# Attention on one core: the value products of a tile's two heads in turn, and scores, maxima, exponentials and scalings branch by branch

## The chip, the cores and the metric

The kernel runs on 1 core of one Trainium2 chip. The metric is the device time of one execution in microseconds (us), as the median of several runs. Lower is better.

## The reference, cut to what matters

Two layers on 256 tokens of width 1024: an HGRN2 mixer with its feed-forward, then a sparse attention (16 query heads of 64, 4 key heads, three branches) with its feed-forward. Everything is float32. With 256 tokens all blocks are selected and the window covers everything, so the selected and the windowed branch are plain causal attentions with keys and values of their own; the third branch attends to 15 compressed blocks.

```python
s_s = jnp.einsum('bqhgd,bhqkd->bhgqk', qr, ks_g) * scale
p_s = masked_softmax(s_s, m_s[:, :, None])
o_s = jnp.einsum('bhgqk,bhqkd->bqhgd', p_s.astype(vs_g.dtype), vs_g)
...
p_w = masked_softmax(s_w, m_w)
o_w = jnp.einsum('bhgqk,bkhd->bqhgd', p_w.astype(vw.dtype), vw)
o = g[:, :, 0] * o_c + g[:, :, 1] * o_s + g[:, :, 2] * o_w
```

## The kernel before, in words

Weights come from HBM as one stream of chunks of 1 MB (tile `raw`, four buffers). Most chunks are split into a high and a low part (`wh` on ScalarE, `wl` on VectorE), and each product is three fp32r matmuls (L484 to L486 in `gemm`). The conditioning vectors are products of plain float32 chunks with column tiles of 32 (`adapsg`, `adapsss`, L385); a scheduler puts them between the pieces of the attention.

The attention works on 8 tiles of two heads. A tile's two heads lie on partitions 0 to 63 and 64 to 127, and are called first and second head (`half` 0 and 1). The branches `br` 0 and 1 are the selected and the windowed one, `tt` is the half of the tokens.

`attend_scores(j)`, L1195: for each half of the tokens and each head one score product into a PSUM bank of its own (tile `s`, L1207), with 64 contracted rows; it holds both branches. Then VectorE adds the mask and takes the maxima (L1211, into `Pt` and `mx`), ScalarE takes eight exponentials (called at L1220, recorded at L429) and VectorE scales by the gate over the sum (L1229).

`attend_values(j)`, L1232: for each of the four pairs of head and branch, three 128x128 transposes through PSUM (`ptt`, L1244) and a copy to `PT` (VectorE for the first, L1247; ScalarE for the others, L1249). Then ten products go into one bank `po`, the first head's to its partitions 0 to 63, the second head's to 64 to 127: per head one of 256 columns with the compressed values (`PC`, L1256) and, per branch, one of 256 (L1260) and one of 128 columns (L1262). The stationary operand is 128 rows by 64 columns, so a product fills half of TensorE's columns; `tile_position` names which half. The trace calls such a shape 128\*64. A float32 product runs as two passes, each with a weight load of its own: the trace has two records for one matmul. Last, `po` is split into `hh` and `hl` (L479, L480) for the output product `nso`.

The order of the calls is a table (`ORDER["nsa"]`), but each engine's order is made by a scheduler that follows the order of the program with an offset (`@first("av")` moves the values forward). The banks `s`, `po` and some others share four PSUM buffers (tag `m`), the transposes share three (tag `acc`), `PT` has five buffers.

Of the kernel before, what the change touches and what calls it, by code (L numbers as in the profile page):

```python
# [20 lines left out]
P = 128  # L21
S = 256
D = 1024
# [4 lines left out]
RAW = 4  # chunks loaded ahead  # L28
DEFER = 3  # chunks of a feed-forward's first product taken before rstd is there
XBUFS = 14  # L30
XMOD, XOFF = 5, 9  # every how many halves of a chunk go to the second ring, and until which chunk
PTS = 3  # pairs of heads with probabilities at a time
QACT, KACT = 0x0F, 0xF0  # chunks of the queries' and values' input made on ACT
CSTK = 7  # chunk after which the rest of the constants is loaded
# how far ahead of the program (behind it, if negative) some of the work is issued
PRI = {"gates": -100, "av": 10, "res": 60, "rot": -15, "fh": 60}
EPS = 1e-6
# [5 lines left out]


# conditioning vectors (s shift and scale, g gate) on the tensor engine; the others are row sums on DVE
# [11 lines left out]
# The order of the work. hgrn: D decays, S scores, i/g products, V values. nsa: q queries, G gates, c compression,  # L57
# n norms, w values, x compressed softmax, s scores, v outputs, a conditioning chunk.
# hada, f0, f1: after how many chunks of products each conditioning chunk comes.
# [115 lines left out]
def row_constants():  # L175
    """Row 32 m + h of column block m: ones on the partitions of half h."""
    r = np.zeros((P, 4, P), np.float32)
    for m in range(4):
        for h in range(2):
            r[32 * m + h, m, 64 * h:64 * h + 64] = 1.0  # L180
    return r.reshape(P, 4 * P)


def first(name):
    """What the method issues is moved by PRI in the order of the program."""
    def wrap(f):
        def g(self, *a, **k):
            n = PRI.get(name, 0)
            if not n:
                return f(self, *a, **k)  # L190
            with self.tc.high_priority(offset=n):
                return f(self, *a, **k)
        return g
    return wrap


class K:
# [154 lines left out]
    def ada(self, kind, l, i, t):  # L352
        """Two columns of 128 conditioning values: rows of the chunk against c."""
        nc = self.nc
# [19 lines left out]
    def ada_pe(self, kind, l, i, t):  # L374
        """c against the chunk's rows, summed over the chunks; at the last one the columns."""
        nc = self.nc
# [42 lines left out]
    def act(self, out, in_, func, **kw):  # L419
        """An activation whose function lies in a table set; sets change only between phases."""  # L420
# [17 lines left out]
    def rsqrt_cols(self, v, n, tag):  # L438
        """v ** -0.5 for a few columns, by Newton's method from the exponent."""
# [11 lines left out]
    def rsqrt(self, v, shape, tag):  # L451
        """(v + EPS) ** -0.5, one Newton step after the tables."""
# [13 lines left out]
    def sigmoid(self, out, v, shape):  # L466
        """exp(min(v, 0)) / (1 + exp(-|v|))"""
# [26 lines left out]
    def gemm(self, ps, w, hh, hl, n=256):  # L494
        """ps = sum over k of w[k] (128 x 128) against h[:, k, :n]."""
# [3 lines left out]
    def tiles(self, w):  # L499
        """The 128 x 128 tiles of half a chunk: high and low parts."""  # L500
# [7 lines left out]
    def set_shift(self, hh, hl, l):  # L508
        """Columns 256 and 257 of the moving operand: the shift vector and zeros."""
# [14 lines left out]
    def stat(self, x, m):  # L524
        """Adds the squares of chunk m to the sum over chunks."""
# [10 lines left out]
    def first_stat(self):  # L536
        """rstd of the input."""
# [25 lines left out]
    def stat_end(self, ps=None):  # L563
        """self.rstd = (mean of squares + EPS) ** -0.5 of every token, on all partitions."""
# [17 lines left out]
    def full_chunk(self, hh, hl, m, A, sh, pool):  # L582
        """Chunk m of x * rstd * A + shift, in two parts."""
# [7 lines left out]
    def full_pair(self, which, l, xr, pool, on_act):  # L591
        """The same from x * rstd."""
# [22 lines left out]
    def gemm_deferred(self, ws, h, pool, name, ub=2):  # L615
        """Products with h as it is before rstd: their values times rstd, and the shift's column."""
# [17 lines left out]
    def residual(self, ps, m, gate, nxt):  # L634
        """x_new chunk m = x + gate * y, with what the next products need of it."""
# [20 lines left out]
    def hgrn(self):  # L656
# [3 lines left out]
        with self.tc.tile_pool(name="hg", bufs=1) as gp, self.tc.tile_pool(name="hg2", bufs=2) as g2:  # L660
# [17 lines left out]
            # room of the next operands until their first parts are there  # L678
# [62 lines left out]
    def gemm_tok(self, ps, h, ws):  # L741
        """Tokens on the partitions: h (stationary) against the weights."""
# [9 lines left out]
    def hgrn_decays(self, fs, qs, g2):  # L752
        """X[l]: exp of the log decay from each block's middle; left keys, right queries. X[8]: keys."""
# [41 lines left out]
    def hgrn_scores(self, X, q, g2, i):  # L795
        nc = self.nc
        # scores inside blocks of 32, all levels side by side
# [45 lines left out]
    def hgrn_values(self, ns, As, v, g2, q):  # L843
        """Into q: rms-normalised rows of A^T v times the gain, features on the partitions."""
# [75 lines left out]
    def raw_heads(self, ps, name):  # L920
        """Products of two column tiles off the accumulator, and their squares."""
# [7 lines left out]
    def rotate(self, u, gain, swap, kr, name):  # L929
        """kr = the rotation of u times the gain: halves of a head change places."""  # L930
# [11 lines left out]
    def head_norm(self, pairs, kr, gain=None, kn=None):  # L942
        """Four column tiles: kr times the heads' rstd, kn = u times that and the gain."""
        nc = self.nc
        ps = self.m_tile([P, S], "hs")
        # rows 32 e and 32 e + 1: the two heads of column tile e
# [124 lines left out]
    def cmp_blocks(self, sw, u, kind, Dt, pool):  # L1071
        """Dt[(parity, d), i, (head, block)]: token 16 block + 2 i + parity of a head, plus its position."""
# [122 lines left out]
    def attend_scores(self, j):  # L1195
# [7 lines left out]
        for tt, (o, n) in enumerate(((0, P), (P, S))):  # L1203
            for half in range(2):
                hs = slice(64 * half, 64 * half + 64)
                ps = self.m_tile([P, 2, n], f"s{tt}")
                nc.tensor.matmul(ps, lhsT=self.QR[hs, j, tt * P:tt * P + P], rhs=self.KR[hs, g, :, 0:n],  # L1207
                                 start=True, stop=True)
                for br in range(2):
                    i = half * 4 + br * 2 + tt  # L1210
                    nc.vector.tensor_tensor_reduce(out=Pt[half][:, br, o:o + n], in0=ps[:, br], in1=cs[:, S - n:],  # L1211
# [4 lines left out]
        for half in range(2):  # L1216
            for br in range(2):
# [8 lines left out]
        for half in range(2):  # L1226
            for br in range(2):
# [5 lines left out]
    def attend_values(self, j):  # L1233
# [4 lines left out]
        for half in range(2):  # L1238
            for br in range(2):
                PT[half, br] = self.pt_tile(f"PT{j}_{half}{br}")  # L1240
                pt = self.pp.tile([P, 3, P], F32, tag="acc", bufs=3, name="ptt")
                # columns: keys 0 with tokens 0, keys 0 with tokens 1, keys 1 with tokens 1
# [8 lines left out]
        for half in range(2):  # L1251
            hs = slice(64 * half, 64 * half + 64)
            kv = 2 * g + half
            o = po[hs]
            tpos = (0, 64 * half)
            nc.tensor.matmul(o, lhsT=self.VC[:, g, (j % 4) * 2 + half], rhs=self.PC[g].rearrange("p a b -> p (a b)"),  # L1256
                             start=True, stop=False, tile_position=tpos)
            for br in range(2):
                v = self.V[:, :, br, 64 * kv:64 * kv + 64]
# [124 lines left out]
```

## Time and profile before

| what | value |
|---|---|
| median of 3 runs | 765.33 us (764.39 to 766.17) |
| profiled execution, its span | 764.0 us |
| TensorE (PE) busy in the span | 736.8 us, 96% |
| VectorE (DVE) / ScalarE (ACT) busy | 573.1 us, 75% / 395.2 us, 52% |

The profile's page gives the profiled execution by its span alone; the runs' times include what lies around the span. A busy share is an average over stages; what ends a stage is read from the chain of waits and the timeline. The attention's value products lie between 475 and 546 us of the span.

### The profile page before, as it was taken

To read this page: it belongs to the slowest core of one execution; us is meant where nothing else is said; L and a number is where in the kernel's file an instruction comes from. 1 tells how busy PE (TensorE), PEld (TensorE's weight loads), DVE (VectorE), ACT (ScalarE), POOL (GpSimd) and SP (SyncE) were. 2 spreads that over 40 slices of the span, in tenths; PEclk is the share of its full clock that TensorE was granted. 3 is DMA by queue.
4 is the path that set the end of the run, shared out by engine and by line. 5 is a ranking of instruction groups with operands and counts; after the bars stand their busy time and mean duration, and the time that the engine had idled before them with its cause. 6 is when DMAs were issued, how large, how long until landed. Compare 5 with 4: busy or idle time off the path is not lost.

```text
span 764.0 us, 15991 instructions
## 1 busy us (share of the span) xinstructions
PE 736.8 (96%) x6580; PEld 671.6 (88%) x6580; DVE 573.1 (75%) x1231; ACT 395.2 (52%) x746; POOL 0.6 (0%) x7
## 2 busy tenths in 40 slices
PE   3999999899999999999999899999999999999997
PEld 1999986689999999999996787555799999999997
DVE  5996988469898988987598869668489757565631
ACT  4339856357644544544474644558466444444330
POOL 0000000000000000000000000000000000000000
PEclk9999999799999999999999999999999999999999
DMA  8999745475489796887733942552755555755710
GB/s 330 335 341 355 274 133 210 139 284 203 143 320 377 275 366 266 333 333 285 274 112 97 359 134 74 173 215 109 275 204 182 208 179 206 275 203 205 266 39 21
DMA packets 26571, 174.13 MB, mean 228 GB/s; under 512 B 3201, under 2 KB 4609, under 8 KB 6018
## 3 DMA queue, kind: packets, MB, share of 16 engines
q1 hardware_dynamic: 24912, 170.80, 60.7%
q10 hardware_dynamic: 1586, 2.32, 1.1%
q8 instruction: 51, 0.84, 0.4%
q14 instruction: 22, 0.18, 0.1%
HBM read 170.48 MB, written 1.05 MB: 225 GB/s over the span
## 4 chain that ended last, share of the span: by engine, by line
PE 88%; DVE 5%; ACT 3%; DMA 2%; issue 1%; ACTq 0%; DVEq 0%
PE ff L486 11%; PE ff L485 11%; PE ff L484 11%; PE ffo L484 6%; PE ffo L485 5%; PE ffo L486 5%; PE adapsss L385 2%; PE po L1260 2%; PE ptt L1244 2%; PE s L1207 2%; DVE wl L308 1%; PE q L485 1%; PE nso L484 1%; PE hg_i L748 1%; PE hgo L484 1%; PE q L486 1%
## 5 line engine op out<-in xcount | busy, mean ns | idle before, releaser
L308 DVE TENSOR_TENSOR wl<-raw,wh 128x1024 fp32r<-128x1024 f32 x201 | 244.0, 1222 | 72.7 <-ACT wh L307 72.2
L307 ACT CAST wh<-raw 128x1024 fp32r<-128x1024 f32 x201 | 208.7, 1048 | 152.8 <-PE ff L485 53.0
L486 PE MATMUL ff<-hh,wl 128*128 128x256 f32 (+1 forms) x704 | 198.3, 282 | 0.0
L484 PE MATMUL ff<-hh,wh 128*128 128x256 f32 (+1 forms) x704 | 198.1, 282 | 0.0
L485 PE MATMUL ff<-hl,wh 128*128 128x256 f32 (+1 forms) x704 | 198.1, 282 | 0.0
L486 PEld LDWEIGHTS ff<-hh,wl 128*128 128x128 f32 x704 | 133.1, 189 | 0.0
L485 PEld LDWEIGHTS ff<-hl,wh 128*128 128x128 f32 x704 | 132.7, 189 | 0.3
L484 PEld LDWEIGHTS ff<-hh,wh 128*128 128x128 f32 x704 | 132.6, 189 | 0.1
L484 PE MATMUL ffo<-gh,wh 128*128 128x256 f32 x352 | 99.0, 282 | 0.6 <-DVE x L638 0.6
L485 PE MATMUL ffo<-gl,wh 128*128 128x256 f32 x352 | 98.6, 280 | 0.0
L486 PE MATMUL ffo<-gh,wl 128*128 128x256 f32 x352 | 98.5, 280 | 0.0
L359 DVE CUSTOM_DVE_ANT_0 junk<-raw,crep 128x1024 f32<-128x1024 f32 x64 | 78.1, 1220 | 2.8 <-DMA raw<-in_w 2.2
L484 PEld LDWEIGHTS ffo<-gh,wh 128*128 128x128 f32 x352 | 66.0, 188 | 1.3 <-DVE x L638 1.0
L486 PEld LDWEIGHTS ffo<-gh,wl 128*128 128x128 f32 x352 | 66.1, 188 | 0.0
L485 PEld LDWEIGHTS ffo<-gl,wh 128*128 128x128 f32 x352 | 66.1, 188 | 0.0
L479 ACT CAST gh<-fg 128x256 fp32r<-128x256 f32 x44 | 17.8, 405 | 42.0 <-DVE fg L894 41.4
L429 ACT ACTIVATE Pt<-Pt,nm 128x128 f32<-128x128 f32 x64 | 28.2, 442 | 9.8 <-DVE nm L1215 9.8
L480 DVE TENSOR_TENSOR gl<-fg,gh 128x256 fp32r<-128x256 f32 x44 | 18.6, 422 | 8.2 <-ACT gh L479 8.2
L587 ACT ACTIVATE hh<-t,mod 128x256 fp32r<-128x256 f32 x24 | 11.4, 505 | 24.6 <-DVE t L586 24.6
L429 ACT ACTIVATE fs<-ff 128x256 f32<-128x256 f32 x38 | 14.5, 380 | 15.3 <-PE ff L486 15.3
L638 DVE SCALAR_TENSOR_TENSOR x<-ffo,mod,x 128x256 f32<-128x256 f32 x16 | 7.7, 482 | 18.9 <-PE ffo L486 18.9
L385 PE MATMUL adapsss<-raw,c 128*32 128x512 f32 x128 | 21.1, 632 | 0.8 <-issue 0.8
(324 smaller groups left out, 1497.8 us busy)
## 6 DMA issues: line engine op xcount, KB each, us to landing
raw<-in_w SPq DMA_DIRECT2D x160, 1024.0 KB, 5.6
x<-in_x SPq DMA_DIRECT2D x2, 512.0 KB, 5.0
usq<-huq ACTq DMA_DIRECT2D x16, 64.0 KB, 2.4
out<-x SPq DMA_DIRECT2D x8, 128.0 KB, 1.9
cst<-in_cst ACTq DMA_DIRECT2D x1, 558.0 KB, 7.7
usk<-huk ACTq DMA_DIRECT2D x8, 64.0 KB, 3.9
raw<-in_w SPq DMA_DIRECT2D x1, 512.0 KB, 4.3
rselr<-in_rsel SPq DMA_DIRECT2D x1, 256.0 KB, 2.9
```

The lines of the kernel that those rows point to most:

```text
L307: nc.scalar.copy(wh, u)
L308: nc.vector.tensor_tensor(wl, u, wh.bitcast(F32), op=ALU.subtract)
L359: nc.vector.tensor_tensor_reduce(out=junk, in0=t[:, h * D:(h + 1) * D], in1=self.crep, scale=1.0, scalar=0.0, op0=ALU.mult, op1=ALU.add, a ...
L385: nc.tensor.matmul(self.aps[32 * j:32 * j + 32, :q], lhsT=self.c32[:, k], rhs=t[:, n * D + j * q:n * D + (j + 1) * q], start=k == 0, stop= ...
L429: r = nc.scalar.activation(out, in_, func, **kw)
L479: self.nc.scalar.copy(hi, v)
L480: self.nc.vector.tensor_tensor(lo, v, hi.bitcast(F32), op=ALU.subtract)
L484: mm(ps, lhsT=wh, rhs=hh, start=first, stop=False)
L485: mm(ps, lhsT=wh, rhs=hl, start=False, stop=False)
L486: mm(ps, lhsT=wl, rhs=hh, start=False, stop=last)
L1207: nc.tensor.matmul(ps, lhsT=self.QR[hs, j, tt * P:tt * P + P], rhs=self.KR[hs, g, :, 0:n], start=True, stop=True)
L1244: nc.tensor.transpose(pt[:, e], Pt[half][:, br, e * P:(e + 1) * P], self.c("ident"))
```

## The change

In `attend_values` the ten products of a tile are no longer all of the first head and then all of the second: each step is taken for both heads, one right behind the other, and the pairs are transposed by branch and, inside, by head. In `attend_scores` the two banks of a half of the tokens are taken first and the two score products stand behind each other; maxima, exponentials and scalings run by branch and, inside, by head. Comments were removed too, so most lines have another number: L1207 is now L1208, L1211 is L1213, L1229 is L1231, L1244 is L1246, L1247 and L1249 are L1249 and L1251, and the three lines L1256, L1260 and L1262 are one, L1263. No instruction is added or removed on any of the engines.

```diff
         for tt, (o, n) in enumerate(((0, P), (P, S))):
+            ps = [self.m_tile([P, 2, n], f"s{tt}") for _ in range(2)]
             for half in range(2):
                 hs = slice(64 * half, 64 * half + 64)
-                ps = self.m_tile([P, 2, n], f"s{tt}")
-                nc.tensor.matmul(ps, lhsT=self.QR[hs, j, tt * P:tt * P + P], rhs=self.KR[hs, g, :, 0:n],
+                nc.tensor.matmul(ps[half], lhsT=self.QR[hs, j, tt * P:tt * P + P], rhs=self.KR[hs, g, :, 0:n],
                                  start=True, stop=True)
-                for br in range(2):
+            for br in range(2):
+                for half in range(2):
                     i = half * 4 + br * 2 + tt
...
-        for half in range(2):
-            for br in range(2):
+        for br in range(2):
+            for half in range(2):
                 for tt, (o, n) in enumerate(((0, P), (P, S))):
                     i = half * 4 + br * 2 + tt
                     self.act(Pt[half][:, br, o:o + n], Pt[half][:, br, o:o + n], AF.Exp, scale=0.125,
...
-        for half in range(2):
-            for br in range(2):
+        for br in range(2):
+            for half in range(2):
                 PT[half, br] = self.pt_tile(f"PT{j}_{half}{br}")
...
-        for half in range(2):
-            hs = slice(64 * half, 64 * half + 64)
-            kv = 2 * g + half
-            o = po[hs]
-            tpos = (0, 64 * half)
-            nc.tensor.matmul(o, lhsT=self.VC[:, g, (j % 4) * 2 + half], rhs=self.PC[g].rearrange("p a b -> p (a b)"),
-                             start=True, stop=False, tile_position=tpos)
-            for br in range(2):
-                v = self.V[:, :, br, 64 * kv:64 * kv + 64]
-                nc.tensor.matmul(o, lhsT=v[:, 0], rhs=PT[half, br][:, 0:S], start=False, stop=False,
-                                 tile_position=tpos)
-                nc.tensor.matmul(o[:, P:S], lhsT=v[:, 1], rhs=PT[half, br][:, S:384], start=False, stop=br == 1,
-                                 tile_position=tpos)
+        pc = self.PC[g].rearrange("p a b -> p (a b)")
+        steps = [(None, self.VC[:, g, (j % 4) * 2:(j % 4) * 2 + 2], pc, slice(0, S))]
+        for br in range(2):
+            for e, t in ((0, slice(0, S)), (1, slice(P, S))):
+                steps.append((br, self.V[:, e, br, P * g:P * g + P].rearrange("p (h d) -> p h d", h=2),
+                              slice(0, S) if e == 0 else slice(S, 384), t))
+        for n, (br, w, r, t) in enumerate(steps):
+            for half in range(2):
+                rhs = r if br is None else PT[half, br][:, r]
+                nc.tensor.matmul(po[64 * half:64 * half + 64, t], lhsT=w[:, half], rhs=rhs, start=n == 0,
+                                 stop=n == len(steps) - 1, tile_position=(0, 64 * half))
```

The order of the instructions follows at three places on TensorE. A `PT` name ends in head, branch and a number (PT_10 is second head, branch 0); in a `Pt` or an `s` name the number alone tells buffers apart.

First place, the third tile's value products, about 497 to 501 us of the span. Before:

```order
L1256 MATMUL po<-PC_5655,VC 64x256 x2
L1260 MATMUL po<-PT_00_6249,V 64x256
L1262 MATMUL po<-PT_00_6249,V 64x128
L1260 MATMUL po<-PT_01_6255,V 64x256
L1262 MATMUL po<-PT_01_6255,V 64x128
L1256 MATMUL po<-PC_5655,VC 64x256
L1260 MATMUL po<-PT_10_6261,V 64x256
L1262 MATMUL po<-PT_10_6261,V 64x128
L1260 MATMUL po<-PT_11_6267,V 64x256
L1262 MATMUL po<-PT_11_6267,V 64x128
```

and after the change:

```order
L1263 MATMUL po<-PC_5655,VC 64x256 x4
L1263 MATMUL po<-PT_00_6249,V 64x256
L1263 MATMUL po<-PT_10_6255,V 64x256
L1263 MATMUL po<-PT_00_6249,V 64x128
L1263 MATMUL po<-PT_10_6255,V 64x128
L1263 MATMUL po<-PT_01_6261,V 64x256
L1263 MATMUL po<-PT_11_6267,V 64x256
L1263 MATMUL po<-PT_01_6261,V 64x128
L1263 MATMUL po<-PT_11_6267,V 64x128
```

Before, the first row holds the first heads of two tiles, and all of the second head stands behind all of the first. Now the first row holds both heads of both tiles, and the heads alternate.

Second place, the last tile's score products between the fifth and sixth tile's transposes and values, about 518 to 525 us. Before:

```order
L1256 MATMUL po<-PC_6382,VC 64x256 x2
L1207 MATMUL s_6559<-KR,QR 128x256
L1207 MATMUL s_6563<-KR,QR 128x256
L1260 MATMUL po<-PT_00_6481,V 64x256
L1207 MATMUL s_6567<-KR,QR 128x512
L1262 MATMUL po<-PT_00_6481,V 64x128
L1244 MATMUL ptt<-cst,Pt_0_6386 128x128 x4
L1260 MATMUL po<-PT_01_6487,V 64x256
L1244 MATMUL ptt<-cst,Pt_0_6386 128x128 x2
L1244 MATMUL ptt<-cst,Pt_1_6387 128x128 x3
L1207 MATMUL s_6571<-KR,QR 128x512
L1244 MATMUL ptt<-cst,Pt_1_6387 128x128 x3
```

and after the change:

```order
L1263 MATMUL po<-PC_6382,VC 64x256 x2
L1208 MATMUL s_6559<-KR,QR 128x256
L1208 MATMUL s_6560<-KR,QR 128x256
L1263 MATMUL po<-PC_6382,VC 64x256 x2
L1263 MATMUL po<-PT_00_6481,V 64x256
L1208 MATMUL s_6567<-KR,QR 128x512
L1208 MATMUL s_6568<-KR,QR 128x512
L1246 MATMUL ptt<-cst,Pt_0_6386 128x128 x3
L1246 MATMUL ptt<-cst,Pt_1_6387 128x128 x3
L1246 MATMUL ptt<-cst,Pt_0_6386 128x128 x3
L1263 MATMUL po<-PT_10_6487,V 64x256
L1263 MATMUL po<-PT_00_6481,V 64x128
```

The two score products of 512 columns stood apart, with transposes and values between them; now they stand together.

Third place, the end of the seventh tile's values among the eighth's transposes, about 537 to 542 us. Before:

```order
L1256 MATMUL po<-PC_6382,VC 64x256
L1260 MATMUL po<-PT_01_6609,V 64x256
L1262 MATMUL po<-PT_01_6609,V 64x128
L1244 MATMUL ptt<-cst,Pt_0_6557 128x128
L1256 MATMUL po<-PC_6382,VC 64x256
L1244 MATMUL ptt<-cst,Pt_0_6557 128x128
L1260 MATMUL po<-PT_10_6615,V 64x256
L1244 MATMUL ptt<-cst,Pt_0_6557 128x128
L1262 MATMUL po<-PT_10_6615,V 64x128
L1244 MATMUL ptt<-cst,Pt_0_6557 128x128
L1260 MATMUL po<-PT_11_6621,V 64x256
```

and after the change:

```order
L1263 MATMUL po<-PC_6382,VC 64x256
L1263 MATMUL po<-PT_10_6609,V 64x256
L1263 MATMUL po<-PT_00_6603,V 64x128
L1246 MATMUL ptt<-cst,Pt_0_6557 128x128
L1263 MATMUL po<-PT_10_6609,V 64x128
L1263 MATMUL po<-PT_01_6615,V 64x256
L1246 MATMUL ptt<-cst,Pt_0_6557 128x128 x2
L1263 MATMUL po<-PT_11_6621,V 64x256
L1246 MATMUL ptt<-cst,Pt_1_6558 128x128
L1263 MATMUL po<-PT_01_6615,V 64x128
```

Single transposes stand between the value products here in both orders, so some runs of value products hold one head alone, and others now hold a product of each.

## Rows read from the trace of the kernel before

**Rows 1.** The page: busy time of TensorE, its busy tenths in 40 slices of the span, and the chain that ended last by engine.

```profile
PE 736.8 (96%) x6580; PEld 671.6 (88%) x6580; DVE 573.1 (75%) x1231; ACT 395.2 (52%) x746; POOL 0.6 (0%) x7
PE   3999999899999999999999899999999999999997
PE 88%; DVE 5%; ACT 3%; DMA 2%; issue 1%; ACTq 0%; DVEq 0%
```

**Rows 2.** Busy time by stretch: from and to, length, then busy us (number of records) of PE, PEld (its weight loads), DVE, ACT, POOL, then the granted TensorE clock (1.00 is 2.4 GHz), DMA share, GB/s.

```profile
463.00:475.50 12.50, 11.36 (x69) 7.75 (x68) 11.96 (x67) 7.60 (x33) 0.00 (x0) 1.00 0.18 61
475.50:487.50 12.00, 11.90 (x109) 7.70 (x110) 6.71 (x29) 7.18 (x26) 0.00 (x0) 1.00 0.49 175
...
497.30:509.30 12.00, 12.00 (x89) 8.07 (x88) 8.18 (x37) 7.75 (x33) 0.00 (x0) 1.00 0.49 184
...
518.10:546.00 27.90, 27.90 (x154) 14.89 (x154) 17.52 (x72) 19.29 (x64) 0.00 (x0) 1.00 0.44 179
546.00:560.00 14.00, 14.00 (x117) 13.85 (x118) 8.94 (x14) 7.55 (x12) 0.00 (x0) 1.00 0.48 170
```

**Rows 3.** The chain of waits in three windows, its shares by line: 475.85 to 487.41 us (first and second tile's values), 497.48 to 509.19 us (third and fourth), 518.24 to 545.83 us (fifth to eighth).

```profile
by line: PE po L1260 30.5%; PE ptt L1244 18.3%; PE adapsg L385 16.0%; PE po L1262 12.2%; PE po L1256 10.7%; PE hs L950 5.3%; ACT hry L429 4.1%; ACT PT L1249 3.3%; issue 0.6%
...
by line: PE po L1260 28.8%; PE adapsss L385 17.0%; PE cs L1172 14.6%; PE ptt L1244 13.8%; PE po L1262 12.1%; PE po L1256 10.5%; PE s L1207 3.7%; PE adat L396 3.2%
...
by line: PE po L1260 26.8%; PE ptt L1244 20.8%; PE po L1262 13.4%; PE adapsss L385 13.3%; PE po L1256 12.9%; PE s L1207 12.3%; PE adat L396 2.1%
```

**Rows 4.** The timeline of PE in the third tile's values: start, length, engine, line, operation, tiles, shape, count.

```profile
499.05 0.38 PE L1260 MATMUL po<-PT,V 128*64 128x256 f32 x1
499.05 0.43 PE L1256 MATMUL po<-PC,VC 128*64 128x256 f32 x1
499.26 0.38 PE L1260 MATMUL po<-PT,V 128*64 128x256 f32 x1
499.32 0.38 PE L1256 MATMUL po<-PC,VC 128*64 128x256 f32 x1
499.48 0.27 PE L1262 MATMUL po<-PT,V 128*64 128x128 f32 x1
499.54 0.38 PE L1260 MATMUL po<-PT,V 128*64 128x256 f32 x1
499.59 0.27 PE L1262 MATMUL po<-PT,V 128*64 128x128 f32 x1
499.75 0.38 PE L1260 MATMUL po<-PT,V 128*64 128x256 f32 x1
```

**Rows 5.** The chain of waits in order of time, 518 to 529 us: start, length, engine, tile, line, count of records.

```profile
518.31 1.01 PE po L1256 x4
519.32 0.86 PE s L1207 x3
...
520.75 1.05 PE s L1207 x2
...
524.03 1.05 PE s L1207 x2
...
527.71 0.86 PE po L1260 x4
528.57 0.44 PE po L1262 x4
```

**Rows 6.** The same view, the fifth tile's score products at 495 and 496 us, where the two heads' products stand together.

```profile
494.89 0.63 PE s L1207 x4
...
496.49 1.06 PE s L1207 x4
```

**Rows 7.** The timeline of PE at 530.4 us, where one product of each head comes free at the same time.

```profile
530.39 0.43 PE L1256 MATMUL po<-PC,VC 128*64 128x256 f32 x1
530.40 0.43 PE L1260 MATMUL po<-PT,V 128*64 128x256 f32 x1
530.66 0.38 PE L1256 MATMUL po<-PC,VC 128*64 128x256 f32 x1
530.66 0.38 PE L1260 MATMUL po<-PT,V 128*64 128x256 f32 x1
```

**Rows 8.** The timelines of ACT, DVE and PE, third window: first exponential of the sixth tile with its wait in brackets, that tile's scalings and first transposes; the seventh tile's copies to `PT`, and the value products that read them.

```profile
517.40 0.40 ACT L429 ACTIVATE Pt<-Pt,nm 128x128 f32<-128x128 f32 x1 [4.10 <-DVE nm L1215]
...
521.49 1.93 DVE L1229 TENSOR_SCALAR Pt<-Pt,cf 128x128 f32<-128x128 f32 x8
...
522.10 0.66 PE L1244 MATMUL ptt<-cst,Pt 128*128 128x128 f32 x4
...
533.75 1.21 ACT L1249 COPY PT<-ptt 128x384 f32<-128x384 f32 x3
...
537.11 0.59 PE L1260 MATMUL po<-PT,V 128*64 128x256 f32 x2
```

**Rows 9.** Weight loads (PEld): two of the second head at 480.3 us and eight of four column tiles at 481.5 us, from the timeline; and all loads of L1260 in the groups of instructions (count, busy us, mean ns).

```profile
480.30 0.19 PEld L1256 LDWEIGHTS po<-PC,VC 128*64 128x64 f32 x2
...
481.53 0.16 PEld L385 LDWEIGHTS adapsg<-raw,c 128*32 128x32 f32 x8 [0.17 <-issue]
...
L1260 PEld LDWEIGHTS po<-PT,V 128*64 128x64 f32 x64 | 7.5, 136 | 2.5 <-issue 1.5
```

More of the change, by code (lines that the diff above doesn't have):

```diff
@@ L1203, in attend_scores @@
         for tt, (o, n) in enumerate(((0, P), (P, S))):
+            ps = [self.m_tile([P, 2, n], f"s{tt}") for _ in range(2)]
             for half in range(2):
                 hs = slice(64 * half, 64 * half + 64)
-                ps = self.m_tile([P, 2, n], f"s{tt}")
-                nc.tensor.matmul(ps, lhsT=self.QR[hs, j, tt * P:tt * P + P], rhs=self.KR[hs, g, :, 0:n],
+                nc.tensor.matmul(ps[half], lhsT=self.QR[hs, j, tt * P:tt * P + P], rhs=self.KR[hs, g, :, 0:n],
                                  start=True, stop=True)
-                for br in range(2):
+            for br in range(2):
+                for half in range(2):
                     i = half * 4 + br * 2 + tt
-                    nc.vector.tensor_tensor_reduce(out=Pt[half][:, br, o:o + n], in0=ps[:, br], in1=cs[:, S - n:],
+                    nc.vector.tensor_tensor_reduce(out=Pt[half][:, br, o:o + n], in0=ps[half][:, br], in1=cs[:, S - n:],
                                                    scale=1.0, scalar=-3e38, op0=ALU.add, op1=ALU.max,
@@ L1250, in attend_values @@
         po = self.m_tile([P, S], "po")
-        for half in range(2):
-            hs = slice(64 * half, 64 * half + 64)
-            kv = 2 * g + half
-            o = po[hs]
-            tpos = (0, 64 * half)
-            nc.tensor.matmul(o, lhsT=self.VC[:, g, (j % 4) * 2 + half], rhs=self.PC[g].rearrange("p a b -> p (a b)"),
-                             start=True, stop=False, tile_position=tpos)
-            for br in range(2):
-                v = self.V[:, :, br, 64 * kv:64 * kv + 64]
-                nc.tensor.matmul(o, lhsT=v[:, 0], rhs=PT[half, br][:, 0:S], start=False, stop=False,
-                                 tile_position=tpos)
-                nc.tensor.matmul(o[:, P:S], lhsT=v[:, 1], rhs=PT[half, br][:, S:384], start=False, stop=br == 1,
-                                 tile_position=tpos)
+        pc = self.PC[g].rearrange("p a b -> p (a b)")
+        steps = [(None, self.VC[:, g, (j % 4) * 2:(j % 4) * 2 + 2], pc, slice(0, S))]
+        for br in range(2):
+            for e, t in ((0, slice(0, S)), (1, slice(P, S))):
+                steps.append((br, self.V[:, e, br, P * g:P * g + P].rearrange("p (h d) -> p h d", h=2),
+                              slice(0, S) if e == 0 else slice(S, 384), t))
+        for n, (br, w, r, t) in enumerate(steps):
+            for half in range(2):
+                rhs = r if br is None else PT[half, br][:, r]
+                nc.tensor.matmul(po[64 * half:64 * half + 64, t], lhsT=w[:, half], rhs=rhs, start=n == 0,
+                                 stop=n == len(steps) - 1, tile_position=(0, 64 * half))
         self.split(self.O[0][:, j, :256], self.O[1][:, j, :256], po)
```

## The prediction, made before the result was known

> **What bounds the kernel now.** I read the page first. TensorE is busy 96% of the span, at nine tenths or more in nearly every slice, and holds 88% of the chain that ended last [rows 1]. The table by stretch then says whether this holds where the change sits: from 475.5 to 546 us of the span PE is busy all the time but for 0.1 us in a stretch, at a granted clock of 1.00 (its level of 2.4 GHz), DVE for half to two thirds, ACT likewise; and the output product behind it has PE without a gap too, 14.00 of 14.00 us [rows 2]. So here an engine's microsecond is the kernel's: what PE saves in its order between 475.5 and 546 moves all that follows, unless another engine then comes late. Before 475.5 no value product runs, and DVE is the full engine (11.96 of 12.50 us, [rows 2]); the score part can win nothing there.
>
> How long do the value products hold PE? The chain of waits in three windows says it by its shares for the three lines of `po` [rows 3]: 53.4% of 11.56 us is 6.2 us (tiles one and two), 51.4% of 11.71 is 6.0 (three and four), 53.1% of 27.59 is 14.6 (five to eight). Together 26.8 us.
>
> What is a pass worth? Four passes of 256 columns take 0.86 us, four of 128 columns 0.44 [rows 5]: 0.216 and 0.109 us, and twice that for a product, 0.43 and 0.22. The run of four at 518.31 takes 1.01, so a run between other shapes costs 0.15 us more than its passes (the other shape's results drain, and the first pass waits for its weights). All 160 passes one after another would be 64 x 0.216 + 64 x 0.109 + 32 x 0.216 = 27.7 us, with 20 runs x 0.15 = 3.0 us 30.7. Measured are 26.8: some overlap is there already. The timeline shows where [rows 4]: at 499.05 the second head's first product (L1256) starts together with a pass of the first head (L1260), though in the order it stands four passes behind it. The two halves of the columns run side by side; but the second head's products stand so far behind the first head's that most of both run alone.
>
> **The change, part by part.**
>
> *Value products.* The order now offers both heads all the time. What a pair then takes, the trace shows once, where a product of each head came free together [rows 7]: both start within 0.01 us and both second passes 0.27 later, as one head alone would (0.216 and the 0.05 of a first pass). So a run takes the passes of its longer head plus 0.15. I add that up over the order after the change, as at its first place for tile three: both pairs with `PC` 4 x 0.216 = 0.86, then 0.43 + 0.22 + 0.43 + 0.22 = 1.30, plus 0.15 is 2.31 us; tile four without its `PC` pair 1.45. Together 3.8 for 6.0: **2.3 us less**. For tiles one and two the order has four runs: two `PC` pairs of 0.58, one of 1.23 with a product of the first head alone, one of 2.10 in which the second head has the longer list: 4.5 for 6.2, **1.7 less**. For tiles five to eight there are still 15 runs, because the scheduler goes on putting single transposes between them (third place); several hold one head alone. Their sum: 0.58, 1.01, 0.58, 1.88, 0.80, 0.58, 0.58, 0.80, 0.58, 0.58, 0.37, 0.37, 0.58, 0.58, 1.45 = 11.3 for 14.6: **3.3 less**. Were all paired, the 26.8 would shrink to 13.9 + 3.1 = 17; the order reaches 19.6.
>
> *Score products.* A product's 64 rows are half of the array too, and pairs that stand together run together already: 0.63 us for 256 columns of both heads, 1.06 for 512 [rows 6]. Only the last tile changes (second place): its three runs of 0.86, 1.05 and 1.05 us [rows 5] become 0.63 and 1.06: **1.25 less**.
>
> *Maxima, exponentials, scalings.* The same instructions in another order on DVE and ACT; where the maxima alternate, a bank comes free one maximum later, its twin at the same time. I cost this at nothing in PE's time, since PE waits for banks only before 475.5 and near 515.
>
> *What comes late next.* In the third window the sixth tile's chain has no room: ACT waits 4.1 us for its maxima, the exponentials start at 517.40, DVE's scalings at 521.49, and PE's transposes at 522.10 follow [rows 8]. PE would reach them about 0.5 us earlier than now; I give back 0.2, the rest is covered by the work that moved ahead of them. Later the room is large: the seventh tile's copies end at 534.96, their product starts at 537.11 [rows 8]. There PE comes some 3 us earlier and ACT only about 1, because it works through exponentials and weight casts in front of the copies; that just about closes the gap without a wait. The weight stream has its next chunks loaded by then and moves forward with the products that release it.
>
> Sum: 1.7 + 2.3 + 3.3 + 1.25 - 0.2 = 8.3 us. Of the profiled execution's 764.0 us of span that leaves 755.7; the median of the runs stands 1.3 above that span, so **757.0 us** for 765.33.
>
> *Bounds of the unknown.* Least gain per pair: what the trace already has, that is none; most: full overlap, rows 7. I take the most, as the nearest row is the same shape. For the waits: from none (0.2 us more gain) to a third window that gains nothing in the end (4.3 less).
>
> **The rivals.**
>
> *New waits eat the third window.* ACT is busy 19.29 of 27.90 us there [rows 2] and the copies to `PT` queue behind eight exponentials. If PE only runs into ACT and DVE, just the first two windows' 4.0 us remain: 761.3 us. For it speak the 4.10 us wait and the 0.6 us between scaling and transposes at 522; against it the 2 us of room at 537 [rows 8]. 8%.
>
> *Passes keep the order of the program.* Then a second head's first pass could start only beside the first head's second, and every run would be one pass longer: about 14 of the 21 runs hold both heads, 14 x 0.216 = 3.0 us less gain, 760.0 us. Rows 7 speak against it, with both first passes ahead of both second ones, and so do rows 4, with a product overtaking four passes. This is what the Trainium skill states in "TensorE: Matmul & The Clock Gate", Part 3 (the mechanism): matmuls start and end in the order of the program, and only weight loads are pulled ahead. By that rule, the time is the 760.0; the trace does not agree with it. 4%.
>
> *Weight loads that come out into the open: slower.* Heads in turn means that each load goes to the other half of the columns than the pass that runs. If such a load cannot hide beside the pass, 160 loads of 0.136 us [rows 9] are 21.8 us: 757.0 + 21.8 = 778.8 us. It decides from about 9.8 us on, 0.06 us per load: 8.3 to lose the gain, 1.5 to be seen. Against it: two loads of the second head lie beside the first head's pass at 480.30, and eight loads of four column tiles fit into 0.16 us [rows 9]. The same page of the Trainium skill, same part, says that a load overlaps with running matmuls only where their row groups differ; both heads use all 128 rows, so that rule would give this case, and rows 4 and 9 deny it. 3%.
>
> *Nothing to gain.* If the heads already overlapped wholly, the time would stay at 765.3. The 26.8 us against 30.7 unpaired and 17 paired say that only a quarter to a third of it is there. 3%.
>
> **How the numbers follow.** My forecast 82%, the rivals 8, 4, 3 and 3%. About 0.2% (1.5 us) is what a measurement of this kernel can tell from no change. Forecast, waits and program order lie over 1.5 us below: faster 94%; no change 3%; slower 3%. The range goes from 755.0 (no waits at all, the full pair at runs I counted as single, 1.8 us for the spread of the runs) to 761.0, which takes in the program-order case and nearly all of the waits; what it leaves out is the rest.
>
> **What would show it.** In the changed profile: the chain's share of `po` in the three windows down to about 4.5, 3.8 and 11.3 us; records of both heads in pairs 0.01 us apart from the first product of a tile on; the last tile's 512-column score products 0.01 us apart; the output product `nso` beginning near 537.5 instead of 545.83; everything behind it of the same length. Wrong would be a `po` time near 26 us, weight loads standing between passes, or PE waiting for `PT` or scalings by more than a few tenths of a us in the third window.

## The result, and the profile after

The changed kernel takes 757.59 us (median of 12 runs, 756.35 to 760.37), the kernel before 764.39 (12 runs, 759.4 to 766.17): a ratio of 0.9915, 95% interval 0.9901 to 0.993. That is 5.4 to 7.6 us less; predicted were 8.3 less and 757.0 us. The time is in the range and the direction is right, but the gain was put too high, and a comparison of one profile with the other hides that, as the next views show.

The page of the changed kernel, first its span, then busy time and the chain by engine (before: [rows 1]):

```profile
span 755.3 us, 15991 instructions
PE 727.8 (96%) x6580; PEld 663.9 (88%) x6580; DVE 572.4 (76%) x1231; ACT 394.9 (52%) x746; POOL 0.6 (0%) x7
...
PE 88%; DVE 5%; ACT 3%; DMA 2%; issue 1%; ACTq 0%; DVEq 0%
```

The spans differ by 8.7 us, 764.0 to 755.3, which looks like the 8.3 forecast. Where do they differ? The table by stretch answers (columns as in [rows 2]). First two stretches of the kernel before, ahead of the attention:

```profile
405.00:412.00 7.00, 5.30 (x27) 4.46 (x28) 6.93 (x15) 2.48 (x6) 0.00 (x0) 0.76 0.45 144
447.00:455.00 8.00, 6.28 (x40) 6.18 (x40) 7.36 (x14) 2.40 (x4) 0.00 (x0) 0.79 0.38 128
```

The same places in the changed kernel, then the three windows of the value products and the output product behind them:

```profile
405.00:412.00 7.00, 5.13 (x37) 4.38 (x38) 6.97 (x15) 3.04 (x7) 0.00 (x0) 1.00 0.38 104
446.00:453.00 7.00, 5.20 (x44) 5.04 (x43) 7.00 (x14) 2.79 (x4) 0.00 (x0) 1.00 0.24 74
473.50:485.00 11.50, 11.50 (x113) 6.65 (x113) 6.31 (x26) 7.25 (x26) 0.00 (x0) 1.00 0.36 113
495.00:504.50 9.50, 9.50 (x89) 6.37 (x87) 7.54 (x36) 7.54 (x31) 0.00 (x0) 1.00 0.48 172
513.50:537.20 23.70, 23.70 (x154) 12.34 (x153) 16.75 (x72) 18.90 (x63) 0.00 (x0) 1.00 0.47 187
537.20:551.20 14.00, 14.00 (x117) 13.85 (x117) 9.38 (x15) 7.50 (x12) 0.00 (x0) 1.00 0.58 205
```

Where the order has not changed, the profiled execution of before ran at a granted clock of 0.76 and 0.79 in two stretches, and that of after at 1.00; PE has gaps there in both. So I compare from a mark just behind these stretches, the transposed probabilities over the compressed blocks, first group (`pct`, L1191), to the first output product (`nso`, L484):

```
                     pct       nso       pct to nso   nso to the end
before               463.32    545.83    82.51        218.17
after                460.94    537.13    76.19        218.17
```

6.32 us come from the stretch that the change touches, 2.38 from ahead of it, and what lies behind the output product has kept its length to 0.01 us. In a second execution of the changed kernel (after_again, below) the stretch was 76.18 us long, and its `pct` stood at 463.54, later than in the kernel before (over all runs between 457.49 and 463.54): the 2.38 us ahead of the stretch are chance and no gain of the change.

The chain of waits in the three windows, shares by line, answers to [rows 3] (473.47 to 485.00 us, 494.98 to 504.54, 513.52 to 537.20):

```profile
by line: PE po L1263 49.3%; PE adapsg L385 28.4%; PE ptt L1246 17.8%; PE hs L950 4.9%
...
by line: PE po L1263 39.9%; PE adapsss L385 20.8%; PE ptt L1246 19.6%; PE cs L1172 17.8%; PE s L1208 4.5%; PE adat L396 3.8%
...
by line: PE po L1263 49.7%; PE ptt L1246 23.2%; PE adapsss L385 15.5%; PE s L1208 9.9%; PE adat L396 3.1%
```

That is 5.7, 3.8 and 11.8 us for the value products, 21.3 for 26.8; forecast were 4.5, 3.8 and 11.3. The timeline of the third tile's run, and of a run near 515 us, against [rows 4]:

```profile
494.98 1.09 PE L1263 MATMUL po<-PC,VC 128*64 128x256 f32 x8
495.90 1.48 PE L1263 MATMUL po<-PT,V 128*64 128x256 f32 x16
...
515.39 0.43 PE L1263 MATMUL po<-PC,VC 128*64 128x256 f32 x1
515.40 0.43 PE L1263 MATMUL po<-PT,V 128*64 128x256 f32 x1
515.65 0.38 PE L1263 MATMUL po<-PC,VC 128*64 128x256 f32 x1
515.67 0.38 PE L1263 MATMUL po<-PT,V 128*64 128x256 f32 x1
515.87 0.59 PE L1263 MATMUL po<-PC,VC 128*64 128x256 f32 x2
```

From 494.98 on, 24 passes take what 12 take alone. At 515.39 and again at 515.65 two passes start within 0.02 us of each other, one of either half of the columns, and two passes are left that run one after the other. The chain in order of time shows the same for whole runs (start, length, engine, tile, line, records; against [rows 5, 6]):

```profile
473.54 1.01 PE po L1263 x4
474.55 0.57 PE hs L950 x8
475.11 1.01 PE po L1263 x4
...
482.55 2.45 PE po L1263 x21
...
495.05 2.32 PE po L1263 x24
...
503.05 1.49 PE po L1263 x16
...
513.59 1.01 PE po L1263 x4
514.60 0.86 PE s L1208 x3
515.46 1.01 PE po L1263 x6
516.47 1.06 PE s L1208 x4
```

The runs at 495.05 and 503.05 are those forecast at 2.31 and 1.45. Those of four records at 473.54, 475.11 and 513.59 are not: forecast at 0.58, they take 1.01, the time of four passes one after another.

### The profile page after: what moved, and what is told of

It is laid out like the page before. It is cut to its first block, busy times and chain, and to the rows that moved or that the text cites. A ratio compares the mean times of both kernels' runs of the same rounds, so it can differ in the third digit from the quotient of the medians.

```text
span 755.3 us, 15991 instructions
## 1 busy us (share of the span) xinstructions
PE 727.8 (96%) x6580; PEld 663.9 (88%) x6580; DVE 572.4 (76%) x1231; ACT 394.9 (52%) x746; POOL 0.6 (0%) x7
## 3 DMA queue, kind: packets, MB, share of 16 engines
q10 hardware_dynamic: 1586, 2.32, 1.1%
HBM read 170.48 MB, written 1.05 MB: 227 GB/s over the span
## 4 chain that ended last, share of the span: by engine, by line
PE 88%; DVE 5%; ACT 3%; DMA 2%; issue 1%; ACTq 0%; DVEq 0%
PE ff L486 11%; PE ff L485 11%; PE ff L484 11%; PE ffo L484 6%; PE ffo L485 5%; PE ffo L486 5%; PE po L1263 3%; PE adapsss L385 2%; PE ptt L1246 2%; DVE wl L308 2%; PE s L1208 1%; PE adapsg L385 1%; PE q L485 1%; PE nso L484 1%; PE hg_i L748 1%
## 5 line engine op out<-in xcount | busy, mean ns | idle before, releaser
L484 PE MATMUL ff<-hh,wh 128*128 128x256 f32 (+1 forms) x704 | 198.1, 282 | 0.0
L484 PEld LDWEIGHTS ff<-hh,wh 128*128 128x128 f32 x704 | 132.6, 189 | 0.1
L484 PE MATMUL ffo<-gh,wh 128*128 128x256 f32 x352 | 99.4, 283 | 0.7 <-DVE x L638 0.7
L484 PEld LDWEIGHTS ffo<-gh,wh 128*128 128x128 f32 x352 | 66.1, 188 | 1.8 <-DVE x L638 1.5
L587 ACT ACTIVATE hh<-t,mod 128x256 fp32r<-128x256 f32 x24 | 11.3, 505 | 21.3 <-DVE t L586 21.3
```

Source lines behind the costliest of these rows:

```text
L484: mm(ps, lhsT=wh, rhs=hh, start=first, stop=False)
```

## The experiments

Theories. **A**: passes in the two halves of the columns run at once where the order offers both within PE's reach, PE is the bound, and the three lone runs hold the same head of two tiles. **B**: the gain comes from exponentials and scalings that reach PE earlier. **C**: only neighbours in the order pair. All twelve runs, by the stretch from `pct` to `nso` and by the ratio of the times (12 runs at most each; a single time for two). A stretch is that of one profiled execution; the two of the changed kernel agree to 0.01 us:

```
                     pct to nso   ratio to before, 95% interval
products_alone       77.10        0.9909 (0.9887 to 0.9931)
scores_alone         82.71        0.9992 (0.9977 to 1.0006)
pc_last              80.93        0.9967 (0.9949 to 0.9985)
heads_whole          84.99        1.0022 (1.0003 to 1.0041)
blocks_of_two        78.79        756.29 us, once
one_half             91.03        772.81 us, once
wide_first           75.19        0.9891 (0.9867 to 0.9915)
wide_first_av5       74.41        0.9891 (0.986 to 0.9922)
after_again          76.18        0.9913 (0.9893 to 0.9934)
middle_s7_first      80.49        0.9967 (0.9949 to 0.9984)
middle_s7_mid        82.52        0.9983 (0.9966 to 1.0001)
second_head_first    75.34        0.9899 (0.9874 to 0.9925)
```

**The two halves of the change.** products_alone takes the diff of the change in `attend_values` and not in `attend_scores`, scores_alone the other way round.

> The kernel before with the value products of a tile's two heads in turn (and the pairs transposed by branch), but scores, maxima, exponentials and scalings as before. Theory (the two halves of the columns run side by side, and TensorE is the bound): 4.8 us less than before (about 759.6 for 764.4). Worked out from the profile of the changed kernel: from the first value product to the output product it takes 63.65 us for 70.00 before, 6.35 less; of that I take off 1.05 for the last tile's score products that stand apart again, and 0.5 for one run of value products more between them. Rival (the gain comes from the exponentials and scalings, which reach PE earlier): no more than 1 us less.

> The kernel before with the change in the scores, maxima, exponentials and scalings alone; the value products run one head after the other as before. Theory: 1.05 us less for the last tile's two score products of 512 columns side by side, and a few tenths for one run less between shapes: 1.0 to 1.6 us less than before. Rival (the gain comes from this half): 5 to 6 us less.

The stretch of each, from the table by stretch (PE busy, granted clock, DMA share, GB/s), first products_alone, then scores_alone:

```profile
462.75:539.85 77.10, 75.93 (x524) 1.00 0.46 174
461.86:544.57 82.71, 81.24 (x524) 1.00 0.46 169
```

The products alone gain 5.4 us of the 6.3, a little more than the 4.8 expected. The scores alone lose 0.2, where 1.0 to 1.6 less were expected. B is out. The order of scores, maxima and exponentials is worth 0.9 us, but only beside the other half. In scores_alone the two score products of 512 columns do pair (all score products keep PE busy for 13.01 us in place of 13.78 between 470 and 550 us), but the value products take 28.65 for 28.22 and the transposes 15.98 for 15.70, all by the table by stretch, and PE comes to the sixth tile's transposes before its scalings are done:

```profile
521.37 0.94 PE L1246 MATMUL ptt<-cst,Pt 128*128 128x128 f32 x6 [0.19 <-DVE Pt L1231]
```

That gives the gain back. The 0.19 us are the lack of room that the prediction saw in the sixth tile's chain.

**How far apart two heads may stand.** pc_last puts the step with the compressed values last, and so keeps a tile's products nearly in one piece; heads_whole and blocks_of_two are pc_last with the second head's first pass ten and four passes behind the first head's.

```diff
-        steps = [(None, self.VC[...], pc, slice(0, S))]
+        pcs = (None, self.VC[...], pc, slice(0, S))
+        steps = []
...
+        steps.append(pcs)
```

```diff
-        for n, (br, w, r, t) in enumerate(steps):
-            for half in range(2):
+        for a in (0, 2, 4):              # heads_whole: one block of all five steps
+            for half in range(2):
+                for n, (br, w, r, t) in list(enumerate(steps))[a:a + 2]:
```

> The changed kernel, but the product with the compressed values is each tile's last step, no longer its first. In the changed kernel three runs hold the first step of the same head of two tiles, or start with it, and their passes run one after the other (1.01 us for four passes). Theory: with that step last, the order keeps a tile's ten products nearly unbroken; by runs of the longer head plus 0.15 us the value products take 4.2 + 3.9 + 9.2 = 17.3 us for 21.3, and 6 runs of transposes less save 0.9: 5 us less than the changed kernel, about 752.6. Rival (the early step is what fills PE's time while PT and the scalings come): 756 to 759, with waits of PE on ACT or DVE between 473 and 537 us.

> As pc_last, but all five steps of the first head and then all five of the second: the second head's first pass stands ten passes behind the first head's. Theory (TensorE reaches some four passes ahead into the other half of the columns, as the trace of before shows at 499.05 us, and no further): a tile then takes 3.46 us for its twenty passes less the 0.65 of the first head's last four, plus 0.15, that is 2.96 for 1.88; over eight tiles 8.6 us more than pc_last. If the reach has no limit: as pc_last. If only neighbours pair: 11 to 13 us more.

> As pc_last, but the heads change after every two steps: the second head's first pass stands four passes behind the first head's, for two in pc_last and ten in heads_whole. To be read in the third tile's unbroken run of 20 passes (1.88 us in pc_last, 3.01 in heads_whole). Theory (TensorE reaches four passes ahead into the other half of the columns): 1.9 to 2.0 us. Rival (it reaches two passes ahead): each block loses 0.43 us at its start, 2.3 us or more. Rival (neighbours only): about 3 us.

The third tile's run of all ten products, by the chain: pc_last, heads_whole, blocks_of_two (18 of heads_whole's 20 records lie on the chain).

```profile
497.44 1.88 PE po L1265 x20
```

```profile
496.87 3.01 PE po L1266 x18
```

```profile
490.94 1.93 PE po L1266 x20
```

Two and four passes apart make no difference, ten passes do: C is out, and so is a reach without limit. The timeline of heads_whole shows where it ends:

```profile
497.72 0.65 PE L1266 MATMUL po<-PT,V 128*64 128x256 f32 x4
498.15 0.38 PE L1266 MATMUL po<-PC,VC 128*64 128x256 f32 x1
498.21 0.38 PE L1266 MATMUL po<-PT,V 128*64 128x256 f32 x1
```

Of the four passes from 497.72, three are the first head's sixth to eighth. The fourth is the second head's first: its next stands at 498.21, and a head's second pass follows its first by 0.27 [rows 7], so it began at 497.94, when the first head's seventh had just begun. The eleventh pass of the order starts with the seventh: four ahead, as at 499.05 us in the kernel before [rows 4]. It had no data to wait for: the last copy to `PT` before it ended at 492.12. Worked out, the 1.14 us from the first head's first pass (496.80) to there, plus 1.73 for the second head, plus 0.15 is the 3.0 us measured. Over the whole stretch heads_whole takes 4.06 us more than pc_last and not the 8.6 expected: its value products hold PE for 6.4 us more (26.62 for 20.24, between 470 and 550 us), but its longest wait is 3.72 us for 4.62 and its mean clock 0.98 for 0.96.

But pc_last as a whole is 4.7 us longer in the stretch than the changed kernel, for all that its value products keep PE busy for 20.24 us in place of 22.74. The wait of the rival in its expectation came, and cost more than the rival had put down (762.44 us for 756 to 759). The timeline, and then the table by stretch:

```profile
535.97 2.99 PE L1246 MATMUL ptt<-cst,Pt 128*128 128x128 f32 x12 [4.62 <-DVE Pt L1231]
```

```profile
531.50:536.00 4.50, 0.03 (x1) 0.91 0.87 315
536.00:539.00 3.00, 3.00 (x13) 0.50 0.55 227
539.00:542.00 3.00, 3.00 (x7) 0.50 0.02 5
542.00:546.00 4.00, 4.00 (x34) 0.99 0.00 0
```

The last tile's score products now begin 64.2 us behind `pct` (55.5 in the changed kernel), at 527.37. Its first transpose comes 8.6 us after that, behind maxima, exponentials and scalings. With the other tiles' products packed together ahead of that PE has nothing left to do: it waits 4.62 us, and then works for 6 us at a granted clock of 0.50 (its level of 1.2 GHz), which costs some 3 us more. blocks_of_two waits just as long at the same place, but its clock is back sooner; by the granted clock that costs 1.7 us for pc_last's 3, which makes up much of its lead of 2.1 us in the stretch:

```profile
529.28 2.97 PE L1246 MATMUL ptt<-cst,Pt 128*128 128x128 f32 x12 [4.62 <-DVE Pt L1231]
```

```profile
529.28:533.00 3.72, 3.72 (x14) 0.54 0.44 185
```

**Is it the halves of the columns?** one_half lets all products with `PT` write the first half.

```diff
-                nc.tensor.matmul(po[64 * half:64 * half + 64, t], ..., tile_position=(0, 64 * half))
+                c = 64 if br is None and half else 0
+                nc.tensor.matmul(po[c:c + 64, t], ..., tile_position=(0, c))
```

> As pc_last, in the same order of heads and steps, but all the products with PT write the first half of the columns, the second head's too (its results are then added to the first head's; only its product with the compressed values stays in the second half). Theory (two halves of the columns are what lets two passes run at once): the third tile's run takes 12 x 0.216 + 8 x 0.109 = 3.5 less 0.02 for its products with PT and the first head's with the compressed values, that is 2.60 + 0.43 + 0.15 = 3.2 us for 1.88. Rival (what counts is that the heads take turns, for the weight loads or the PSUM writes): 1.9 us.

The scheduler took the third tile's run apart here, so the forecast run is not there. The run of five products that begins the first tile is, in the same order: first one_half, then pc_last.

```profile
478.20 1.88 PE po L1266 x10
```

```profile
479.50 1.23 PE po L1265 x10
```

Ten passes one after the other are 6 x 0.216 + 4 x 0.109 = 1.73, plus 0.15, 1.88. Heads in turn give nothing by themselves; the two halves do it. In one_half both heads also write the same place in PSUM, which could force one pass behind the other too. The lone runs of the changed kernel speak against that: their passes go to one half of the columns but to two PSUM banks, and take 1.01 us, one after the other, all the same.

**The lone runs.** second_head_first turns the heads of one step of one tile round, and TensorE's rows stay as they were.

```diff
-            for half in range(2):
+            for half in ((1, 0) if br is None and j == 1 else (0, 1)):
```

> The changed kernel, but the second tile's first step takes its second head first; TensorE's rows stand as in the changed kernel, one for one. There the two lone runs with the compressed values hold the first heads of tiles one and two, then the second heads, and take 1.01 us each (four passes one after the other). Now each holds one head of each kind. Theory (two passes run at once only in different halves of the columns, and any two that stand together there pair, of whatever tile): 0.58 us each, 0.86 us less between the first transposes and the output product: 75.3 us for 76.2. Rival (lone runs with the same moving data, or of two PSUM banks, never pair): 1.01 us each, 76.2.

```profile
472.26 0.58 PE po L1263 x4
472.84 0.57 PE hs L950 x8
473.41 0.58 PE po L1263 x4
```

0.58 for 1.01, twice, as theory A has it, and 75.34 us for the stretch, 0.85 less. The two products of such a run are of two tiles and two PSUM banks and pair all the same.

**Versions that go further.** wide_first makes the first step one product over all 128 columns; wide_first_av5 also lowers the values' offset to 5.

```diff
-        steps = [(None, self.VC[...], pc, slice(0, S))]
+        c0 = (j % 4) * 2
+        steps = []
+        nc.tensor.matmul(po, lhsT=self.VC[:, g, c0:c0 + 2].rearrange("p h d -> p (h d)"), rhs=pc, start=True, stop=False)
```

> The changed kernel, but the first step of a tile, which has the same moving data for both heads, is one product over all 128 columns in place of two of 64. It needs no partner. Theory: the lone runs with the compressed values (1.01 + 1.01 us for tiles one and two, 1.01 for five and six) need half of their passes: about 1.5 us less in the value products than the changed kernel, 0.3 less for two runs of transposes; 7.5 to 8.5 us less than before (ratio 0.990). Rival (the shape of 128 columns ends a run, at 0.15 us each, and the lone runs were hidden anyway): as the changed kernel, 6.5 us less.

> As wide_first, with the offset that moves the values forward at 5 in place of 10. By the order fewer single transposes stand between the value products: 19 runs of them for 21 and 19 of transposes for 24. Theory (PE is the bound): counted by runs it takes 3.6 us less than the changed kernel, 10 less than before (ratio 0.987). Rival (as in pc_last, PE then runs into the scalings): waits of PE for DVE of 2 us and more between 513 and 545 us, no better than the changed kernel.

Both are ahead of the changed kernel, by 1.0 and 1.8 us in the stretch. That is less than the 1.8 and 3.6 counted; score products then stand alone more often (17.65 us of PE between 460 and 547 for 16.93) and one waits 0.5 us for maxima. The waits of 2 us and more that the rival of wide_first_av5 feared did not come. By the times alone the intervals overlap those of after_again, and the same is so for second_head_first: all three are faster than the kernel before, and only the trace puts them ahead of the changed kernel.

> The changed kernel once more, beside the next two on one chip. 6.3 us less than before from the fifth query's transposed row (pct) to the output product, and as much in the time, if what differs ahead of that stretch is chance.

The stretch is 6.33 us shorter than before, and the time 6.3 us (758.55 for 764.82). The next two pack the products more tightly still.

> The changed kernel with three edits in the order: the step with the compressed values third in place of first, values not moved forward (offset 0 for 10), and the eighth tile's scores ahead of the fifth's and sixth's values. By the order every tile's products stand in one or two runs (10 runs for 21), and 9.6 us of TensorE's work lie between the eighth tile's last score product and its first transpose, for 3.7 in pc_last, where the wait was 4.6, so that some 8.3 are needed. Theory (PE is the bound, and pc_last lost by that wait alone): counted by runs 7.7 us less than the changed kernel, about 14 less than before (750 for 764.8). Rival (maxima, exponentials and scalings of the tiles cannot keep that pace, or the weight stream can't): waits of PE of 3 to 5 us, 753 to 756.

> As middle_s7_first, but with the eighth tile's scores between the fifth's and the sixth's values: 8.4 us of TensorE's work between its last score product and its first transpose. Theory: 0.8 us more than middle_s7_first by runs, no wait over 0.5 us in the eighth tile. Rival as there.

```diff
-PRI = {..., "av": 10, ...}
+PRI = {..., "av": 0, ...}
-        "... s6 v4 v5 s7 a v6 a a "
+        "... s6 s7 v4 v5 a v6 a a "      # middle_s7_mid: s6 v4 s7 v5
...
+        steps.insert(2, (None, self.VC[...], pc, slice(0, S)))
```

The value products get shorter (19.27 us of PE in middle_s7_first, the least of all runs, and 20.27 in middle_s7_mid, for 22.74 in the changed kernel), and the stretch gets longer by 4.3 and 6.3 us. My rule for the eighth tile held, and the waits came elsewhere. First PE waits 1.50 us for maxima, in both versions, and from 519 to 522 us it works at a granted clock of 0.50 (0.52 in middle_s7_mid). Then, in middle_s7_first, it waits for the copies to `PT`, which stand in ACT's queue behind the exponentials of three tiles. The timeline and the clock of middle_s7_first:

```profile
518.55 4.65 PE L1208 MATMUL s<-KR,QR 64*128 64x512 f32 x12 [1.50 <-DVE mx L1213]
...
530.57 1.11 PE L1264 MATMUL po<-PT,V 128*64 128x256 f32 x4 [2.45 <-ACT PT L1251]
```

```profile
530.00:533.00 3.00, 2.43 (x15) 0.50 1.04 426
533.00:536.00 3.00, 3.00 (x15) 0.50 0.56 238
```

In middle_s7_mid the longest wait is 3.2 us, on DVE's copy to `PT`. So the theory is wrong for both. The rival's waits came, and its price was too low (762.02 and 763.67 us for 753 to 756).

## Why the prediction was right, and where it was not

**PE as the bound: right.** In the third window it is busy for 23.70 of 23.70 us, and all that lies behind the first output product moved up whole.

**A run takes the passes of its longer head plus 0.15 us: right.** 2.32 and 1.49 for tiles three and four (2.31 and 1.45 forecast), and 14 of the 15 runs forecast for the third window came within 0.07 us. one_half and pc_last show the rule without and with the second half of the columns. What makes up the 0.15 us no run here takes apart. The rival that passes keep the order of the program is out by the pairs at 515.39; what is left of it is a reach of four passes. The Trainium skill says in "TensorE: Matmul & The Clock Gate", Part 3 (the mechanism), that matmuls start in the order of the program; heads_whole shows the eleventh starting with the seventh, so here it holds only within one half of the columns.

**The step that failed: "two `PC` pairs of 0.58".** I read two neighbouring rows with the compressed values as the two heads of one tile. They are the same head of two tiles, as second_head_first shows: the turn of one tile's heads brings both runs to 0.58. The excess is 2 x 0.43 us in the first window and 0.43 in the third, 1.3 of the 2.0 us by which the sum was too high; second_head_first settles the 0.86, and the 0.43 rest on the same reading. Another 0.35 us are missing in the first window, in the run of 2.45 (2.10 forecast): ACT's last copy to `PT` waits 0.27 us there until a product has left a `PT` buffer,

```profile
483.38 0.48 ACT L1251 COPY PT<-ptt 128x384 f32<-128x384 f32 x1 [0.27 <-PE po L1263]
```

and ends at 483.86 with its product next; a run with more `PT` buffers was not made, so that this is the whole cause is argued, not shown.

**Score products: 1.04 for 1.25.** The 1.05 + 1.05 became 1.06 as forecast, but the run of 0.86 stays [rows 5]. Its two products stood behind each other in the order before the change too (second place), and the second starts 0.26 us after the first in both kernels; the 0.63 forecast for it came from another place [rows 6].

**Maxima, exponentials, scalings at nothing: right**, to within the 0.2 us of scores_alone. **The sixth tile's 0.2: not needed**, PE waits for nothing there in the changed kernel; in scores_alone the wait is there, with 0.19.

**New waits in the third window** did not come with this change. They were the right thing to fear: pc_last and the middle versions lose more to them than the tighter packing brings. Single transposes and lone first steps between the products, which I had counted only as a cost (0.15 us a run), may also give the other engines time. But they are not all that keeps the waits away: wide_first_av5 has fewer single transposes and half the passes in the first steps, and no wait over 0.7 us. Its last tile's score products begin 54.2 us behind `pct` (55.5 in the changed kernel), and those of pc_last and blocks_of_two, where PE waits 4.62 us, 64.2 and 63.1. No run moves that place alone, so that it decides is argued, not shown. **Weight loads in the open** are out: 24 passes in the time of 12 leave no place for them.

The ledger: forecast 1.7 + 2.3 + 3.3 + 1.25 - 0.2 = 8.3; measured 0.5 + 2.2 + 2.8 + 1.0 = 6.5 by the chain, beside 6.32 for the whole stretch. By the medians the gain is 6.8, 1.5 less than forecast; that the time is only 0.6 us off is luck: the median of before was 0.9 us lower in these runs than in those that the forecast started from. Luck too is the output product at 537.13, near the 537.5 that was to show it: 2.38 us of that come from ahead of the stretch.

## What to carry to other kernels

Put products that fill different halves of TensorE's columns within four passes of each other, and look up which half each product of a run fills: two neighbours of the same kind can be the same head of two tiles. Before work is packed together, ask whose wait it covered. In the five runs with the longest waits (2.45 to 4.62 us) PE's clock fell too, and the wait was in part paid again. Compare two profiles from a mark behind the last stretch in which their clocks differ.

## What the runs showed of the hardware

PE reached four passes ahead into the other half of the columns (heads_whole), across tiles and PSUM banks (second_head_first). One transpose between them, a matmul of another shape, ends that. The chain of the changed kernel at the third place of the order has a product of the second head, one transpose and a product of the first head, three passes behind the first of these, and all run one after the other:

```profile
531.13 0.58 PE po L1263 x2
531.71 0.26 PE ptt L1246
531.97 0.36 PE po L1263 x2
```

After a wait of 4.62 us the clock was granted at 0.50 for 6 us of full work in pc_last, and then at 0.99 again; after the same wait in blocks_of_two it was back within 3.7 us (0.54 in the mean of these), so that one such wait had two prices. one_half waits 1.98 us at 530 and 1.28 us at 542, and its clock stays at 1.00; middle_s7_first waits 1.50 us and its clock falls. The length of the wait alone does not tell.
